# First four feature-column products of a decoder layer made before the norm: r and shift applied at the PSUM read, modulation weights laid out by feature tile

## The chip, the cores and the metric

The kernel runs on one core of a Trainium2 chip. The metric is the device time of one execution in microseconds (us), the median of several. Engines: PE is TensorE (matmul; PEld its weight load), DVE is VectorE, ACT is ScalarE, POOL is GpSimd, SP is SyncE, whose queue issues the DMAs.

## The reference, cut to what matters

A decoder layer for 1024 prompt tokens and 8 decode tokens (T = 1032 columns), D = 1024 features. The part before the token mixers:

```python
mod = (silu(c) @ w_ada + b_ada)                    # 6 x 1024 values: sh1, sc1, gt1, sh2, sc2, gt2
h = rmsnorm(x, g_pre_mix) * (1 + sc1) + sh1        # rmsnorm: x * r(token) * g, r = 1/sqrt(mean(x*x) + eps)
proj = h @ w_in                                    # 1024 -> 2048, in 16 tiles of 128 columns
a_val, a_gate, b_in, c_u, c_v, d_b, d_c, d_h = split(proj, 8)
za = a_val * sigmoid(a_gate)                       # tiles 0, 1 times tiles 2, 3; then a causal conv, 31 taps
...
x = x + gt1 * rmsnorm(out @ w_out, g_post_mix)     # then a SwiGLU FFN with its own norms and modulation
```

The prompt has one c, each decode token its own; so sh1 and sc1 have nine columns per feature.

## The kernel before, in words

Everything is transposed: features lie on the 128 partitions, tokens in the free direction. x is held as KD = 8 feature tiles `xk[k]` of 128 x 1032. The tokens are taken in three column groups c = 0, 1, 2 of W = 344 (the last eight of c = 2 are the decode tokens). Every fp32 product is made of three matmuls: operands are split into a rounded part and a rest (`hh`/`hl`, `wh`/`wl`), and `mm3` (L183 to L188) multiplies hh·wh, hl·wh and hh·wl into one PSUM bank. PSUM has six rotating banks (`psum`) and one double one (`psum_two`). The order of the work on each engine is the order in which the Python code issues it; there is no scheduler, and each engine takes its own queue in order.

The front of the program: all eight x tiles are loaded (`x_load`, L119). ACT squares them and DVE adds the squares into `Sx` (`x_stat`, L369 to L376). `compact_r` (L316) sums over the partitions with matmuls by `ones` (L325), makes r by Newton steps on DVE, spreads it by diagonal matrices `dg` (L336) and matmuls (L338), and ACT copies it to `rx` (L379). The modulation comes in slices of two feature tiles: four pieces of 512 KB each, `ada_mm` (L216 to L220, 32 small matmuls per slice), a copy (`ada_evac`, L224), a turn (`ada_turn`, L229) and `ada_finish` (L232), which leaves sh1 in `mod` and g·(1 + sc1) in `gmul["g1"]`. `modulate_steps` (L402) then makes, for a tile and a column group, tmp = x·G·r on DVE (L405), hh = tmp + sh on ACT (L408) and hl on DVE (L409); for c = 2 POOL does the eight decode columns (L413 to L417).

The first four weight tiles (`IN_ORDER` = 2, 0, 3, 1: gates and values of the conv mixer) are multiplied for c = 0 and most of c = 1 while the modulation still arrives: seven accumulators (five banks and the double one) grow by two feature tiles per slice s (the loop over s, `accs` and `ks`). Then come projection (1, 1) (tile 1, c = 1), five blocks of `v_units` (L628: 128 tokens x 256 columns of w_v, 24 matmuls a block), in whose cover the c = 2 tiles are modulated, the four c = 2 projections, the other four blocks, and the other projections from (6, 0) on. `gate` (L530) and `value` (L535) read the accumulators from PSUM. `ada_rest` makes the remaining modulation slices and `conv_a` (L543) the conv chain on DVE (L550, 58 links) as side generators that `step()` advances between pieces of TensorE work. `compact` (L889) makes the later norms the same way as `compact_r`. `split` (L140) rounds a weight block on ACT (L145) and makes its rest, mostly on POOL (L146).

## Time and profile before

| | |
|---|---|
| median of 3 runs | 1079.89 us (1078.48 to 1080.2) |
| profiled execution, its own time | 1080.22 us |
| span from its first to its last instruction | 1078.5 us |
| busy: PE, DVE, ACT, POOL | 1028.6, 728.7, 373.0, 378.3 us |
| moved by DMA | 169.54 MB, 157 GB/s in the mean |

Times in the rows are us from the start of the span, durations of groups in ns where the view says so. A busy PE is not PE at full speed: the granted clock stands in a row or column of its own. In the timeline a row gives start, duration, engine, line, operation, tiles; in brackets the idle time before it and what ended it. An idle engine costs something only where another waits for its work.

### The profile page before, as it was taken

Reading aid. Unit: us, or ns where it says so; the run is one execution under the profiler, and the core shown is the slowest. Engines: PE = TensorE matmul, PEld = TensorE weight load, DVE = VectorE, ACT = ScalarE, POOL = GpSimd, SP = SyncE. Lnnn points to the kernel's source line nnn. Section 1 sums busy time; section 2 is a strip of 40 time slices with the busy share of each in tenths; the row PEclk is TensorE's granted clock in tenths of the full one; section 3 lists DMA queues with packets and bytes.
Section 4 is the critical chain, followed back from the end, with each engine's and each line's share of the span. In section 5 each row is a group of like instructions: output and inputs, shape, how many; then the busy total and the mean of one; then the engine's idle time right before and its main releaser. Section 6 shows DMA issues by size and latency. Waiting matters only on the chain.

```text
span 1078.5 us, 21308 instructions
## 1 busy us (share of the span) xinstructions
PE 1028.6 (95%) x8658; PEld 1003.7 (93%) x8658; DVE 728.7 (68%) x1318; ACT 373.0 (35%) x732; POOL 378.3 (35%) x338
## 2 busy tenths in 40 slices
PE   4998999999998999999999999999999999999995
PEld 3897888899998899999999999999999999999994
DVE  5483978998336897697666666666667674539476
ACT  4240022114433333333323323323225463436431
POOL 1251144423534433443333323323333344315240
PEclk9999999999998999999999999999999999999997
DMA  9812434572323320256344444344338895646423
GB/s 355 306 41 79 156 112 145 132 176 66 112 79 118 133 92 14 69 183 210 139 167 148 138 168 147 138 168 148 138 128 305 313 322 181 190 157 218 157 89 149
DMA packets 69091, 169.54 MB, mean 157 GB/s; under 512 B 14200, under 2 KB 16128, under 8 KB 68992
## 3 DMA queue, kind: packets, MB, share of 16 engines
q1 hardware_dynamic: 68992, 168.17, 46.1%
q8 instruction: 68, 1.11, 0.4%
q14 instruction: 31, 0.25, 0.1%
HBM read 127.21 MB, written 40.93 MB: 156 GB/s over the span
## 4 chain that ended last, share of the span: by engine, by line
PE 72%; DVE 13%; issue 6%; DMA 3%; ACT 3%; POOL 3%; SPq 0%; POOLq 0%; DVEq 0%; ACTq 0%
PE ps L186 20%; PE ps L187 20%; PE ps L188 20%; PE ps L220 2%; PE pc L187 2%; PE pc L188 2%; PE pc L186 2%; DVE sq L915 1%; DVE pc L550 1%; DMA draw<-a 1%; POOL m L951 1%; PE ps L641 1%; PE ps L642 1%; PE ps L643 1%; DMA adas<-in_wada 1%
## 5 line engine op out<-in xcount | busy, mean ns | idle before, releaser
L186 PE MATMUL ps<-thP,sP 128*128 128x256 f32 (+1 forms) x1064 | 299.7, 282 | 0.7 <-DVE u L1176 0.7
L187 PE MATMUL ps<-tlP,sP 128*128 128x256 f32 (+1 forms) x1064 | 299.6, 282 | 0.0
L188 PE MATMUL ps<-thP,sP 128*128 128x256 f32 (+1 forms) x1064 | 299.4, 281 | 0.0
L186 PEld LDWEIGHTS ps<-thP,sP 128*128 128x128 f32 x1064 | 200.3, 188 | 1.2 <-DVE u L1176 1.1
L188 PEld LDWEIGHTS ps<-thP,sP 128*128 128x128 f32 x1064 | 200.6, 189 | 0.0
L187 PEld LDWEIGHTS ps<-tlP,sP 128*128 128x128 f32 x1064 | 200.3, 188 | 0.0
L186 PE MATMUL ps<-dt,ds 128*128 128x256 f32 (+1 forms) x484 | 136.6, 282 | 0.0
L187 PE MATMUL ps<-dt,ds 128*128 128x256 f32 (+1 forms) x484 | 136.2, 281 | 0.0
L188 PE MATMUL ps<-dt,ds 128*128 128x256 f32 (+1 forms) x484 | 136.1, 281 | 0.0
L1014 POOL TENSOR_TENSOR sP<-ssum,sP 128x512 fp32r<-128x512 f32 x57 | 75.6, 1327 | 147.1 <-ACT sP L1012 145.5
L1265 POOL TENSOR_TENSOR ds<-draw,ds 128x512 fp32r<-128x512 f32 x42 | 71.6, 1707 | 117.1 <-ACT ds L1259 115.0
L186 PE MATMUL ps<-hh,wh 128*128 128x344 f32 x300 | 100.2, 334 | 1.3 <-ACT hh L408 1.2
L187 PE MATMUL ps<-hl,wh 128*128 128x344 f32 x300 | 96.7, 322 | 0.4 <-DVE hl L409 0.4
L188 PE MATMUL ps<-hh,wl 128*128 128x344 f32 x300 | 96.5, 322 | 0.0
L1012 ACT CAST sP<-ssum 128x512 fp32r<-128x512 f32 x76 | 45.4, 620 | 138.4 <-DVE ssum L1047 70.7
L186 PEld LDWEIGHTS ps<-dt,ds 128*128 128x128 f32 x484 | 91.2, 188 | 0.0
L187 PEld LDWEIGHTS ps<-dt,ds 128*128 128x128 f32 x484 | 91.1, 188 | 0.0
L188 PEld LDWEIGHTS ps<-dt,ds 128*128 128x128 f32 x484 | 91.1, 188 | 0.0
L550 DVE SCALAR_TENSOR_TENSOR pc<-za,vec,pc 128x1024 f32<-128x1024 f32 x58 | 74.6, 1286 | 1.4
L1264 DVE TENSOR_TENSOR dt<-draw,dt 128x520 fp32r<-128x520 f32 x77 | 63.9, 854 | 15.7 <-ACT dt L1258 15.6
L1258 ACT CAST dt<-draw 128x520 fp32r<-128x520 f32 x77 | 48.2, 626 | 61.6 <-PE pc L188 40.4
L146 POOL TENSOR_TENSOR wl<-wr,wh 128x1024 fp32r<-128x1024 f32 x14 | 33.6, 2401 | 89.7 <-ACT wh L145 83.0
(319 smaller groups left out, 2432.4 us busy)
## 6 DMA issues: line engine op xcount, KB each, us to landing
wr<-in_wada SPq DMA_DIRECT2D x32, 512.0 KB, 3.9
t<-tsum SPq DMA_DIRECT2D x22, 520.0 KB, 3.1
draw<-t SPq DMA_DIRECT2D x44, 260.0 KB, 5.4
wraw<-in_w_gate SPq DMA_DIRECT2D x22, 512.0 KB, 4.6
wraw<-in_w_up SPq DMA_DIRECT2D x22, 512.0 KB, 5.1
dsum<-in_w_down SPq DMA_DIRECT2D x22, 512.0 KB, 5.6
draw<-s SPq DMA_DIRECT2D x44, 256.0 KB, 5.3
draw<-in_w_down SPq DMA_DIRECT2D x33, 256.0 KB, 5.3
```

Source lines behind the costliest of these rows:

```text
L146: (lo_eng or nc.gpsimd).tensor_tensor(out=lo, in0=raw, in1=hi.bitcast(F32), op=ALU.subtract)
L186: nc.tensor.matmul(out, wh, xh, start=start, stop=False, skip_group_check=more)
L187: nc.tensor.matmul(out, wh, xl, start=False, stop=False, skip_group_check=more)
L188: nc.tensor.matmul(out, wl, xh, start=False, stop=stop, skip_group_check=more)
L220: nc.tensor.matmul(acc[32 * g:32 * g + 32, :P], csil[:, k, :], piece[:, kk, g, :], start=(k == 0), stop=(k == KD - 1))
L550: nc.vector.scalar_tensor_tensor(out=acc if j < 30 else ca[i][:, :SEQ], in0=za[i][:, j:j + SEQ], scalar=v(VCAW + 31 * i + j), in1=acc, op0 ...
L641: nc.tensor.matmul(ps[:m, :GW], hh[k][:, tk], w[0][:, k % 4], start=(k == 0), stop=False)
L1012: nc.scalar.copy(out=t[:, 0], in_=src)
L1014: eng.tensor_tensor(out=t[:, 1], in0=src, in1=t[:, 0].bitcast(F32), op=ALU.subtract)
L1258: nc.scalar.copy(out=t[:, 0], in_=x[:, 1])
L1264: V.tensor_tensor(out=t[:, 1], in0=x[:, 1], in1=t[:, 0].bitcast(F32), op=ALU.subtract)
L1265: (V if k % 2 else nc.gpsimd).tensor_tensor(out=s[:, 1], in0=x[:, 0, :512], in1=s[:, 0].bitcast(F32), op=ALU.subtract)
```

## The change

The products of the first four weight tiles no longer wait for r and for the shift. With G = g·(1 + sc1) and shift sh, W·(x·G·r + sh) = r·(W·(x·G)) + W·sh. So hh/hl first hold the parts of x·G alone (`gained`). Ten extra columns behind c = 1 (`EXTRA`, NX = 10) hold the parts of sh1 itself (nine values and one of padding), and the c = 1 accumulators, 354 columns wide, give W·sh1 in them (`take_bias`). When PSUM is read, DVE multiplies by r (`with_r`) and the bias is added in the sigmoid or in the value's product.

The modulation weights of this part are laid out by feature tile: 16 pieces of 512 KB, a scale and a shift piece for each k, in six rotating buffers. `ada_first` makes the nine (ten) values of a piece with eight small matmuls, an ACT copy and one matmul by `sel`, all in one PSUM bank. x and w_first are loaded tile by tile as well. The sums of squares run beside the products. For all later consumers (v blocks, projections from (6, 0) on) the eight tiles are made a second time, now with r and shift: `scaled` (x·G·r in place: odd k by DVE, even k by POOL and ACT) and `shifted` (hh on ACT, hl on DVE), while projections (1, 0), (2, 2), (0, 2), (3, 2), (1, 2) run. The nine v blocks then stand together, two to a bank. The sums in `compact_r` and `compact` are 8 columns wide instead of 128.

```diff
+        def ada_first(k, what):
+            piece = first_pieces.pop((k, what))
+            acc = psum()
+            for kk in range(2):
+                for g in range(4):
+                    nc.tensor.matmul(acc[32 * g:32 * g + 32, :P], csil[:, 2 * g + kk, :], piece[:, 2 * g + kk, :], start=(kk == 0), stop=(kk == 1))
+            st = sm.tile([P, P], F32, tag="ada", name="ada", bufs=1)
+            nc.scalar.copy(out=st, in_=acc[:, :P])
+            yield
+            tp = acc[:, 256:288]
+            nc.tensor.matmul(tp, st, sel, start=True, stop=True)
...
+            if what:
+                nc.vector.tensor_scalar(out=sh1t[:, k], in0=tp[:, :NX], scalar1=b, scalar2=None, op0=ALU.add)
+            else:
+                t = sm.tile([P, 9], F32, tag="nt", name="nt")
+                nc.vector.tensor_scalar(out=t, in0=tp[:, :9], scalar1=b, scalar2=1.0, op0=ALU.add, op1=ALU.add)
+                nc.vector.tensor_scalar(out=gmul["g1"][:, k], in0=t, scalar1=v(VGPRE + k), scalar2=None, op0=ALU.mult)
...
+        def gained(k, src, dst):
+            nc.scalar.mul(out=hh[k][:, dst], in_=xk[k][:, src], mul=G1[:, k, 0:1])
+            nc.vector.scalar_tensor_tensor(out=hl[k][:, dst], in0=xk[k][:, src], scalar=G1[:, k, 0:1], in1=hh[k][:, dst].bitcast(F32),
+                                           op0=ALU.mult, op1=ALU.subtract)
+        def parts(src, k, dst, eng):
+            nc.scalar.copy(out=hh[k][:, dst], in_=src)
+            eng.tensor_tensor(out=hl[k][:, dst], in0=src, in1=hh[k][:, dst].bitcast(F32), op=ALU.subtract)
+        def scaled(k, cl, r, eng):
+            x = xk[k][:, cl]
+            if eng is nc.vector:
+                eng.scalar_tensor_tensor(out=x, in0=x, scalar=G1[:, k, 0:1], in1=r, op0=ALU.mult, op1=ALU.mult)
+            else:
+                eng.tensor_tensor(out=x, in0=x, in1=r, op=ALU.mult)
+                nc.scalar.activation(out=x, in_=x, func=AF.Identity, scale=G1[:, k, 0:1], bias=sh1(k)[:, 0:1])
+        def shifted(k, cl, eng):
+            x, hi, lo = xk[k][:, cl], hh[k][:, cl], hl[k][:, cl]
+            if eng is nc.vector:
+                nc.scalar.activation(out=hi, in_=x, func=AF.Identity, bias=sh1(k)[:, 0:1])
+                nc.vector.scalar_tensor_tensor(out=lo, in0=x, scalar=sh1(k)[:, 0:1], in1=hi.bitcast(F32), op0=ALU.add, op1=ALU.subtract)
+            else:
+                nc.scalar.copy(out=hi, in_=x)
+                nc.vector.tensor_tensor(out=lo, in0=x, in1=hi.bitcast(F32), op=ALU.subtract)
+        def eng_of(k):
+            return nc.vector if k % 2 else nc.gpsimd
...
-        accs = [(IN_ORDER[j], 0) for j in range(4)] + [(IN_ORDER[j], 1) for j in range(3)]
+        accs = [(n, 0) for n in (2, 3, 0)] + [(n, 1) for n in (2, 3, 0, 1)]
...
-        for s in range(4):
+        for k in range(KD):
             for j, (n, c) in enumerate(accs):
...
+                mm3(first[n, c][:, :gw(c)], w_in[n](k), gx(k, c), k == 0, k == KD - 1)
+                if k < KD - 1:
...
+                    if j == (3 if k == 0 else 1):
+                        g = ada_first(k + 1, 0)
+                        next(g)
+                    if j == (4 if k == 0 else 3):
+                        next(g, None)
+                        gained(k + 1, LO, LO)
+                    if j == 4:
+                        g = ada_first(k + 1, 1)
+                        next(g)
+                        for q in ((k + 1,) if k < 3 else (4, 5) if k == 3 else range(k + 2, min(k + 3, KD))):
+                            x_stat(q)
+                    if j == 6:
+                        next(g, None)
+                        parts(sh1t[:, k + 1], k + 1, EXTRA, nc.gpsimd)
+                if k == 6 and j == 3:
+                    comp = compact_r(Sx, 2 * W, rx_out(rx), big.tile([P, 6, P], F32, tag="y12", name="dg"))
+                    next(comp)
+                    next(comp)
...
+        def with_r(ps, c):
+            t = sm.tile([P, W], F32, tag="tmp", name="tmp", bufs=4)
+            nc.vector.tensor_tensor(out=t, in0=ps[:, :W], in1=rx[:, cols(c)] if c < 2 else rx2, op=ALU.mult)
+            return t
...
+        evac(2, 0)
+        evac(3, 0)
+        next(comp)
+        gained_proj(1, 0)
+        evac(0, 0)
+        gained_proj(2, 2)
+        evac(2, 1)
+        evac(3, 1)
+        for k in range(KD):
+            scaled(k, LO, rx, eng_of(k))
...
+        gained_proj(0, 2, comp)
...
+            shifted(k, LO, eng_of(k))
+        gained_proj(3, 2)
...
+        gained_proj(1, 2)
+        CL2 = slice(2 * W, SEQ)
+        for k in range(KD):
+            scaled(k, CL2, rx2[:, :NP2], eng_of(k))
...
-                nc.tensor.matmul(ps[:, P * b:P * b + P], S[:, t0:t0 + P], ones, start=True, stop=True)
+                nc.tensor.matmul(ps[:, 8 * b:8 * b + 8], S[:, t0:t0 + P], ones[:, :8], start=True, stop=True)
```

**The order on PE, at the start.** Before: the sums over tokens (`ones`, `Sx`), a whole modulation slice, its turn and the diagonals stand ahead of the first product of `hh` and `wh`.

```order
L325 MATMUL ps<-ones,Sx 128x128 x6
L220 MATMUL ps<-adas,csil 32x128 x32
L229 MATMUL ps<-ident,ada 128x128
L338 MATMUL ps<-dg,ones 128x128 x5
L338 MATMUL ps<-dg,ones 128x48
L186 MATMUL ps<-hh_147,wh 128x344
```

In the change one piece (eight matmuls) and its turn stand ahead of it (lines are those of the changed kernel; `w_140` is the first w_first tile):

```order
L224 MATMUL ps<-adas,csil 32x128 x8
L229 MATMUL ps<-sel,ada 128x32
L185 MATMUL ps<-hh_97,w_140 128x344
L186 MATMUL ps<-hl_105,w_140 128x344
L187 MATMUL ps<-hh_97,w_140 128x344
L224 MATMUL ps<-adas,csil 32x128 x8
```

The sums and diagonals have moved behind the products of the seventh and into those of the last feature tile.

**The order on DVE, in the tile loop** of the change (one tile's period; `g_93` is G, `hl_107` the rest of tile 2):

```order
L232 TENSOR_SCALAR sh1t<-ps,vec 128x10
L235 TENSOR_SCALAR nt<-ps,vec 128x9
L236 TENSOR_SCALAR g_93<-nt,vec 128x9
L400 SCALAR_TENSOR_TENSOR hl_107<-x_73,g_93,hh_99 128x688
L386 TENSOR_TENSOR Sx<-Sx,sqx 128x688
```

The sums of squares, which stood ahead of everything, have moved into the loop, behind the rest of each tile and ahead of the next read of a shift.

**The order on POOL, in the second modulation** of the change (`rx_116` is rx2, r for the last 344 columns):

```order
L413 TENSOR_TENSOR x_71<-x_71,rx 128x688
L413 TENSOR_TENSOR x_73<-x_73,rx 128x688
L413 TENSOR_TENSOR x_75<-x_75,rx 128x688
L413 TENSOR_TENSOR x_77<-x_77,rx 128x688
L413 TENSOR_TENSOR x_71<-x_71,rx_116 128x336
```

These are new: before, POOL multiplied only the eight decode columns of a tile. On DVE stand at the same time the odd tiles' `L411` (688 columns, x and rx as inputs) and the eight `L421`/`L424` of the shifted tiles.

## Rows read from the trace of the kernel before

**Rows 1.** The page, part 1: busy us, share of the span and instructions of each engine.

```profile
PE 1028.6 (95%) x8658; PEld 1003.7 (93%) x8658; DVE 728.7 (68%) x1318; ACT 373.0 (35%) x732; POOL 378.3 (35%) x338
```

**Rows 2.** Busy time by stages: stretch, its length, then PE, PEld, DVE, ACT, POOL busy (instructions), granted clock, DMA share, GB/s.

```profile
0.00:10.00 10.00, 0.00 (x0) 0.00 (x0) 3.40 (x6) 5.81 (x8) 0.20 (x4) 1.00 0.81 270
10.00:20.00 10.00, 5.73 (x80) 4.94 (x81) 5.97 (x19) 3.41 (x5) 2.35 (x1) 1.00 1.03 403
20.00:30.00 10.00, 8.29 (x93) 6.98 (x92) 5.47 (x14) 4.23 (x8) 2.37 (x1) 0.83 1.03 409
...
100.00:120.00 20.00, 18.08 (x188) 15.75 (x189) 13.74 (x32) 0.27 (x1) 0.88 (x3) 0.91 0.48 160
...
140.00:160.00 20.00, 20.00 (x188) 17.99 (x187) 13.47 (x15) 4.66 (x9) 12.43 (x11) 1.00 0.31 106
```

**Rows 3.** PE's timeline from 13 to 66: the sums over tokens, the turn of a slice, the first product, products at either level of the clock, the end of projection (1, 1), a v block (every third row of its products).

```profile
13.68 2.93 PE L325 MATMUL ps<-ones,Sx 128*128 128x128 f32 x12 [13.68 <-DVE Sx L376]
...
19.50 0.33 PE L229 MATMUL ps<-ident,ada 128*128 128x128 f32 x1 [0.38 <-ACT ada L224]
...
23.16 0.42 PE L186 MATMUL ps<-hh,wh 128*128 128x344 f32 x1 [1.21 <-ACT hh L408]
...
24.74 0.49 PE L187 MATMUL ps<-hl,wh 128*128 128x344 f32 x1
25.02 0.49 PE L188 MATMUL ps<-hh,wl 128*128 128x344 f32 x1
...
30.54 0.32 PE L188 MATMUL ps<-hh,wl 128*128 128x344 f32 x1
30.70 0.32 PE L186 MATMUL ps<-hh,wh 128*128 128x344 f32 x1
...
64.07 0.83 PE L325 MATMUL ps<-ones,Sx 128*128 128x128 f32 x6
...
65.10 0.28 PE L641 MATMUL ps<-whx,hh 128*128 128x256 f32 x1
...
65.45 0.28 PE L641 MATMUL ps<-whx,hh 128*128 128x256 f32 x1
```

**Rows 4.** The chain of waits, 0 to 125: start, length, what.

```profile
10.60 7.83 DMA adas<-in_wada
...
98.63 3.25 DMA wr<-in_wada
101.92 0.71 PE ps L220 x16
...
117.82 0.57 PE ps L220 x16
118.39 0.35 PE ps L186
```

**Rows 5.** The DMA view, 0 to 60: GB/s in 40 slices of 1.5 us.

```profile
GB/s 0 179 299 301 334 402 409 376 418 410 401 423 401 407 415 401 421 393 410 412 404 412 410 407 419 369 377 338 316 350 359 168 0 76 273 0 0 0 0 5
```

**Rows 6.** Groups of instructions, 0 to 130, by line and shape: count, busy us, mean ns of one, idle before.

```profile
L409 DVE SCALAR_TENSOR_TENSOR hl<-tmp,mod,hh 128x344 fp32r<-128x344 f32 x16 | 8.5, 574 | 1.3 <-ACT hh L408 1.3
L376 DVE TENSOR_TENSOR Sx<-Sx,sqx 128x688 f32<-128x688 f32 x7 | 6.1, 875 | 3.6 <-ACT sqx L375 3.1
L336 DVE TENSOR_SCALAR dg<-ident,nr 128x128 f32<-128x128 f32 x9 | 2.2, 282 | 1.3 <-PE ps L338 1.3
L408 ACT ACTIVATE hh<-tmp,mod 128x344 fp32r<-128x344 f32 x16 | 8.6, 582 | 10.9 <-DVE tmp L405 10.9
L145 ACT CAST whx<-wr 128x1024 fp32r<-128x1024 f32 x2 | 2.0, 1038 | 0.0
L224 ACT COPY ada<-ps 128x128 f32<-128x128 f32 x6 | 1.6, 265 | 41.5 <-PE ps L220 41.5
```

**Rows 7.** POOL's timeline from 70 to 80 (two products of the decode columns), and the DVE row beside the first.

```profile
70.59 0.52 POOL L414 TENSOR_TENSOR td<-td,rx 128x8 f32<-128x8 f32 x1 [4.67 <-ACT rx L379]
...
79.41 0.20 POOL L414 TENSOR_TENSOR td<-td,rx 128x8 f32<-128x8 f32 x1
...
70.49 1.05 DVE L405 SCALAR_TENSOR_TENSOR tmp<-x,g,rx 128x336 f32<-128x336 f32 x2 [1.03 <-ACT rx L379]
```

**Rows 8.** Single lines with the least, median and greatest duration in ns, and three rows of the timeline: POOL's wlx, and a later pair on POOL and DVE.

```profile
L376 DVE TENSOR_TENSOR Sx<-Sx,sqx x14: 517/875/2534, 6.5 to 60.3; 128x688 f32<-128x688 f32 x7, 128x344 f32<-128x344 f32 x7
L1014 POOL TENSOR_TENSOR sP<-ssum,sP x57: 1285/1297/1894, 435.4 to 813.9; 128x512 fp32r<-128x512 f32 x57
...
59.85 5.21 POOL L146 TENSOR_TENSOR wlx<-wr,whx 128x1024 fp32r<-128x1024 f32 x2 [10.36 <-ACT whx L145]
826.62 1.72 POOL L1265 TENSOR_TENSOR ds<-draw,ds 128x512 fp32r<-128x512 f32 x1 [1.20 <-ACT ds L1259]
827.10 1.79 DVE L1264 TENSOR_TENSOR dt<-draw,dt 128x520 fp32r<-128x520 f32 x1
```

**Rows 9.** PE's timeline at a later compact (two column sums of 128 columns, then the next product) and at two 8-column fp32 matmuls.

```profile
294.95 0.60 PE L895 MATMUL ps<-ones,sq 128*128 128x128 f32 x4
295.31 0.36 PE L186 MATMUL ps<-ya,whx 128*128 128x256 f32 x1
...
185.75 0.28 PE L732 MATMUL ps<-td,poolw 128*128 128x8 f32 x2
185.89 0.40 PE L186 MATMUL ps<-hh,wh 128*128 128x344 f32 x1
```

More of the change, by code (lines that the diff above doesn't have):

```diff
@@ L329, in compact_r @@
             small_rsqrt(m9[:, :nb], nb, r9[:, :nb], 1.0 / D, RMS_EPS)
-            yield
+            for b in range(nb):
+                nc.vector.tensor_scalar(out=dg[:, b], in0=ident, scalar1=r9[:, b:b + 1], scalar2=None, op0=ALU.mult)
             for b0 in range(0, nb, 4):
+                yield
                 ps = psum()
@@ L334, in compact_r @@
                 for b in range(b0, min(b0 + 4, nb)):
-                    dg = sm.tile([P, P], F32, tag="dg", name="dg")
-                    nc.vector.tensor_scalar(out=dg, in0=ident, scalar1=r9[:, b:b + 1], scalar2=None, op0=ALU.mult)
                     skip = P * b - offs[b]
-                    nc.tensor.matmul(ps[:, w0:w0 + P - skip], ones, dg[:, skip:], start=True, stop=True)
+                    nc.tensor.matmul(ps[:, w0:w0 + P - skip], ones, dg[:, b, skip:], start=True, stop=True)
                     w0 += P - skip
@@ new lines, in build, with x_square @@
+        G1 = gmul["g1"]
+        Sx = big.tile([P, 2 * W], F32, tag="y13", name="Sx")
+        Sx2 = sm.tile([P, W], F32, tag="tmp", name="Sx2", bufs=4)
+        rx = sm.tile([P, 2 * W], F32, tag="nw", name="rx", bufs=1)
+        rx2 = const.tile([P, W], F32, tag="p3", name="rx2")
+        hd = const.tile([P, KD, ND], F32, name="hd")
+        LO, EXTRA, HI2 = slice(0, 2 * W), slice(2 * W, 2 * W + NX), slice(2 * W, T)
+        NP2 = W - ND
+        def x_square(k, S, cl, sq, eng):
+            if k == 0:
+                nc.scalar.activation(out=S, in_=xk[k][:, cl], func=AF.Square)
+            else:
+                nc.scalar.activation(out=sq, in_=xk[k][:, cl], func=AF.Square)
+                eng.tensor_tensor(out=S, in0=S, in1=sq, op=ALU.add)
@@ L493, in build @@
+                if k == 7 and j == 6:
+                    comp = compact_r(Sx2, W, rx_out(rx2), sm.tile([P, 3, P], F32, tag="tmp", name="dg", bufs=4))
+                    next(comp)
+        gained(KD - 1, slice(2 * W, SEQ), slice(2 * W, SEQ))
+        nc.gpsimd.tensor_tensor(out=hd, in0=hd, in1=G1[:, :, 1:9], op=ALU.mult)
+        for k in range(KD):
+            parts(hd[:, k], k, slice(SEQ, T), nc.gpsimd)
         sgut = load([P, 4, P], a["sgut"], "sgut", "p0")
@@ L628, in v_units @@
         def v_units(wv):
[L629 removed]
+            for grp in ((0, 1, 2, 3), (4, 5, 6, 7), (8,)):
                 ng = len(grp)
@@ L800, in build, with gained_proj, evac @@
         fns = {2: gate(0), 0: value(0), 3: gate(1), 1: value(1)}
-        for n, c in ((2, 0), (3, 0), (2, 1), (3, 1), (0, 0), (1, 0), (0, 1)):
-            proj(n, c, fns[n])
-        proj(1, 1, fns[1])
+        def gained_proj(n, c, g=None):
+            ps = first[n, c] = psum()
+            for k in range(KD):
+                if k == 3 and g is not None:
+                    next(g, None)
+                mm3(ps[:, :W], w_in[n](k), gx(k, c), k == 0, k == KD - 1)
+        def evac(n, c):
+            fns[n](first.pop((n, c)), c)
+        for n in (2, 3, 0, 1):
+            take_bias(n)
+        evac(2, 0)
+        evac(3, 0)
+        next(comp)
+        gained_proj(1, 0)
[3 more added lines that the diff above has]
+        evac(3, 1)
+        for k in range(KD):
+            scaled(k, LO, rx, eng_of(k))
+        evac(0, 1)
+        evac(1, 1)
+        evac(1, 0)
+        gained_proj(0, 2, comp)
+        for k in range(4):
+            shifted(k, LO, eng_of(k))
+        for k in range(4, KD):
+            shifted(k, LO, eng_of(k))
+        gained_proj(3, 2)
+        evac(2, 2)
+        evac(0, 2)
+        evac(3, 2)
+        gained_proj(1, 2)
+        CL2 = slice(2 * W, SEQ)
+        for k in range(KD):
+            scaled(k, CL2, rx2[:, :NP2], eng_of(k))
+        nc.gpsimd.tensor_tensor(out=hd, in0=hd, in1=rx2[:, None, DS].to_broadcast([P, KD, ND]), op=ALU.mult)
+        nc.gpsimd.tensor_tensor(out=hd, in0=hd, in1=sh1t[:, :, 1:9], op=ALU.add)
+        evac(1, 2)
         c_start()
```

320 lines of the change are left out of this document (142 added, 178 removed).

## The prediction, made before the changed kernel had run

> **What bounds the kernel now.** I read the page first: TensorE is busy 95% of the span, the other engines 35 to 68% [rows 1]. What is left to gain lies at the start, so the table by stages comes next: no TensorE work in the first 10 us, 5.73 in the second 10, a clock of 0.83 in the third, and short idle or slow stretches up to 120 [rows 2]. Then TensorE's timeline [rows 3]: the first product of a feature tile starts at 23.16, projection (1,1) ends at 64.07. The chain of waits says why it starts so late: a modulation piece lands at 18.4 [rows 4]; the sums over tokens, which waited for DVE until 13.68, the turn, the diagonals and rx all stand ahead of the first product [rows 3]. In the same chain the first product of projection (6,0), after which the program hardly differs, starts at 118.39. My sum is made up to there, in the profiled execution (1080.22 us by its own time, span 1078.5; the median of the runs is 0.33 lower).
>
> **The head start.** Ahead of the first product the change leaves 1.45 MB of loads (c, vec, ident, the decode columns, one x, one w_first piece, one modulation piece). The bandwidth row gives 0.27, 0.45, 0.45 and 0.50 MB in the slices of 1.5 us up to 7.5 [rows 5], so they are in at 6.9. Then eight small matmuls (0.57, [rows 4]), copy (0.27), turn (0.33) [rows 3, 6], two small DVE operations (estimated 0.4), the ACT write of hh (0.58) [rows 6] and hops: first product at about 9.4. **Gain 13.7 us.**
>
> **The tile loop.** The number of products stays: 21 per tile. At full clock they follow each other in 0.157, at the lower level (1.2 GHz) in 0.286 [rows 3]. TensorE has just been idle, so tile 0 is paid at 0.286, with its second piece in between: 8.3 us. Later tiles cost TensorE 21 × 0.157 + 2 × 0.57 (pieces, [rows 4]) + 0.2 = 4.65. But one PSUM bank (five hold accumulators, two more belong to the double one) serves both pieces of a tile, so the steps form a ring: shift read out by DVE 0.2, piece 0.67, six products 0.95, turn 0.3, gain on DVE 0.45, ACT hh of 688 columns 0.86, DVE hl 0.93, DVE sum of squares 0.88, and the shift's read again. The 0.86 and 0.93 are estimates: 2 × the 0.53 at which 344-column operations follow each other [rows 7] less one fixed part; the 0.88 is a row [rows 6]. Together 5.25, with two sums in tiles 3 and 4 0.9 more. So tile 7's gain is turned at T = 48.9. **About 8 us of the head start go here** (3.7 in tile 0, 0.6 in each later one, and the two sums).
>
> **The tail of the tiles.** In DVE's queue stand hl of tile 7, the Newton steps (12 × an estimated 0.2) and six diagonals (6 × 0.28 at most, [rows 6]) ahead of tile 7's shift; its extra columns come 2.3 late. The second group of diagonal matmuls needs the bank that ACT's first rx copy frees, and seven ACT operations of up to 0.58 [rows 6] stand before it: 1.8. The sums for the last 344 columns wait for the second rx copy, behind two weight casts of 1.04 [rows 6]: 1.4. Projection (1,0) needs a bank that DVE frees only after the rx copies, four bias copies and one product with rx: 1.9. With the work between, it starts at T + 15.85 and ends at T + 19.6 = 68.5, where before stood at 64.07 [rows 3]. **Here 13.7 of gain have become a loss of 4.4.**
>
> **The second modulation.** LO (688 columns) and the last 336 of all eight tiles are made again, with r and shift, before the v blocks. Four projections of 24 × 0.157 = 3.77 cover it: the first v block could end at T + 38.6. The work: POOL multiplies four tiles of 688 and four of 336 columns. No POOL multiply of that size is in the trace; at the 1.29 of its 512-column ones [rows 8] I take 1.72 and 0.85, 10.3 together. DVE has four scaled tiles and eight shifted ones of about 0.93 and the value products: 12 from T + 24, when POOL has done wlx (2 × 2.4) and the decode columns. Can these run at once? A DVE sum (L376, 344 columns) that takes 0.52 alone took 2.53 in the stretch of POOL's wlx; DVE's L1264 took 1.79 beside a POOL L1265 that took 1.72, where POOL needs 1.3 for 512 columns [rows 8]. A POOL product of eight columns took 0.52 while DVE's L405 ran, and 0.20 when DVE had done with them [rows 7]. So the two exclude each other in the one form (tensor_tensor) in both directions, and POOL waits for the other (scalar_tensor_tensor); whether that other form waits for a long POOL operation no row shows. If all of it goes one by one, hl of tile 7 is there at T + 24 + 10.3 + 12 = T + 46.5, and the first v block ends at T + 47, 8 late; if only the tensor_tensor half waits, at T + 40.5, 2 late. I take the first, since the rows nearest to it (L405, L409 against L414) are of that form. The Trainium skill ("SBUF — State Buffer", section "Who interferes with whom") says that a DVE instruction with two SBUF inputs contends with a GpSimd instruction that reads SBUF, and that whoever issues first holds the pair of ports for the whole instruction. By that rule all of it goes one by one; it speaks against giving half of the tiles to POOL.
>
> From there eight more v blocks of 24 × 0.118 = 2.85 [rows 3], some seven pieces of 0.57 [rows 4] and a stretch at the lower clock, as after the stall of 98.63 to 101.92 [rows 4], where 16 small matmuls still took 0.71: 2 us. T + 47 + 22.8 + 4 + 2 = 124.7. **Projection (6,0) starts at about 125 instead of 118.39: +6.5.**
>
> **What costs nothing or little.** The compacts' sums become 8 columns wide: a 128-column one takes 0.18 (two in 0.36), an 8-column one 0.14 [rows 9], and the later compacts have 30 by the code; 30 × 0.04 = **−1.2**, from 0 to at most 30 × 0.18 = −5.4. The ten extra columns: 96 × 0.157 × 10/344 = 0.4, counted in the 4.65. The conv chain on DVE (each link 1.286) starts some 6 us later; DVE is idle for 6.5 us in 140 to 160 [rows 2], which covers it; without them they would come on top. The pieces' loads: 16 × 512 KB with x and w_first at the 400 GB/s of [rows 5] are in by 39, and the last is needed at 45. SP's queue gets no longer; a fetch of the later slices behind POOL's weight split could repeat the 3.25 stall of [rows 4], which is as long as the one it replaces.
>
> Sum: 1080.22 + 6.5 − 1.2 = 1085.5; less 0.33, **1085 us**. The bounds: if only half of the second modulation waits, 6 less (1079); if the lower clock holds through the gaps of the tile loop, some 8 more (1093).
>
> **Rivals.** *(B) POOL and DVE run side by side.* Then hl of tile 7 comes at about T + 39, 7.5 earlier, there is no stall and no clock loss after it: projection (6,0) starts at 116 and the time is 1076.5, faster. For it: scalar_tensor_tensor is never seen waiting for POOL. Against: [rows 7, 8]. It decides as soon as scaled and shifted operations of DVE keep 0.93 beside POOL's. *(C) The tiles run at TensorE's pace.* If the ring is no longer than 4.65 (the estimated 0.86 and 0.93 would have to be 0.6) and the tail is half as long, T is 44 and projection (1,0) ends at 58: most of the head start is kept and the second modulation has 10 us more, 1069. For it: in 10 of the 20 us behind the first product nothing but the pieces held TensorE up (8.29 busy in 20 to 30, with the late start in it, [rows 2]). Against: before, a whole slice of two tiles was made ahead of need, now one bank and one tile. *(D) The clock falls in the tile loop.* In 20 to 30 it was granted at 0.83 after an idle start [rows 2]; if gaps of 0.6 in every 5.3 us keep products at 0.286, each such tile costs 2.7 more; three or four of them make 1094. Against: 100 to 120 had gaps as well and 0.91.
>
> **How the numbers follow.** The forecast (all serialized) 0.52, B 0.25, C 0.13, D 0.10. A measurement of this kernel can tell about 0.2% (2 us) from no change. Forecast: 0.85 slower, 0.08 same, 0.07 faster; B 0.80 faster, 0.10 same; C nearly all faster; D all slower. That makes faster 0.36, same 0.08, slower 0.56. The range goes from C (1070) to D (1094), since B, C and the unknown half of the second modulation lie inside and about 0.1 is left at either end; the forecast's own is 1079 to 1091.
>
> **What would show it.** Right: first product near 9.4; tile periods of 5.2 to 5.5 with TensorE waiting on hh and hl; a gap before projection (1,0) behind rx; DVE's and POOL's 688-column operations at two or more times their lone duration around 70 to 95; the first v block stalled on hl; projection (6,0) near 125. Wrong: tile periods under 4.8, or (1,0) ending before 62; 688-column DVE operations at 0.93 beside POOL's 1.7; projection (6,0) before 117; a granted clock of half speed through several tiles; or any difference after projection (6,0) beyond the 1.2 of the compacts.

## The result, and the profile after

The changed kernel takes 1093.66 us (median; 1093.48 to 1097.13), the kernel before 1079.57 beside it: 1.0135 times as long, 95% interval 1.0116 to 1.0153. The forecast was 1085.0, slower by 5.4 us. The direction is right, the size is not: the profiled execution takes 1093.53, against 1080.22 that is **+13.3**. Two single executions far above the rest (4491.42 us in run 1, 1134.57 of the kernel before beside run 15) are left out of the ratios.

The page after, part 1 (the same columns as [rows 1]), and the table by stages (as [rows 2]):

```profile
PE 1040.3 (95%) x8686; PEld 1009.6 (92%) x8686; DVE 749.8 (69%) x1329; ACT 391.9 (36%) x791; POOL 391.3 (36%) x344
```

```profile
0.00:10.00 10.00, 1.08 (x16) 0.66 (x16) 0.90 (x3) 2.52 (x4) 1.47 (x5) 1.00 0.76 225
10.00:20.00 10.00, 7.81 (x69) 5.60 (x69) 2.21 (x7) 3.34 (x9) 1.48 (x2) 1.00 1.03 408
20.00:30.00 10.00, 10.00 (x101) 8.55 (x98) 4.25 (x9) 5.05 (x12) 3.00 (x4) 1.00 1.04 402
...
140.00:160.00 20.00, 20.00 (x187) 18.21 (x182) 19.09 (x29) 3.15 (x7) 7.19 (x8) 1.00 0.24 76
160.00:180.00 20.00, 16.95 (x146) 15.14 (x145) 10.54 (x12) 4.52 (x10) 8.42 (x9) 0.91 0.41 138
```

In the first 30 us TensorE does work for 18.9 us where before it did 14.0: the head start is real. But it is now busy in all of 20 to 30, so there is no idle time left there in which added work could hide, and in 140 to 160 DVE is busy for 19.09 of 20 (before 13.47) while a gap opens in 160 to 180.

PE's timeline after, from the first modulation piece to the late gap (start, length, what; in brackets the idle time before and who ended it):

```profile
8.66 1.08 PE L224 MATMUL ps<-adas,csil 128*32 128x128 f32 x16 [8.66 <-DMA adas<-in_wada]
...
11.95 0.66 PE L185 MATMUL ps<-hh,w 128*128 128x344 f32 x1 [1.20 <-ACT hh L399]
...
14.89 0.49 PE L186 MATMUL ps<-hl,w 128*128 128x344 f32 x1
15.18 0.47 PE L187 MATMUL ps<-hh,w 128*128 128x344 f32 x1
...
15.65 0.32 PE L186 MATMUL ps<-hl,w 128*128 128x344 f32 x1
15.81 0.32 PE L187 MATMUL ps<-hh,w 128*128 128x344 f32 x1
...
26.81 0.41 PE L185 MATMUL ps<-hh,w 128*128 128x344 f32 x1
...
27.70 0.32 PE L187 MATMUL ps<-hh,w 128*128 128x344 f32 x1
27.95 0.65 PE L224 MATMUL ps<-adas,csil 128*32 128x128 f32 x16
...
28.79 0.32 PE L186 MATMUL ps<-hl,w 128*128 128x344 f32 x1
...
29.43 0.32 PE L187 MATMUL ps<-hh,w 128*128 128x354 f32 x1
29.59 0.30 PE L229 MATMUL ps<-sel,ada 128*128 128x32 f32 x2
...
29.97 0.33 PE L186 MATMUL ps<-hl,w 128*128 128x354 f32 x1
...
32.17 0.40 PE L185 MATMUL ps<-hh,w 128*128 128x344 f32 x1
...
39.66 0.64 PE L224 MATMUL ps<-adas,csil 128*32 128x128 f32 x16 [0.85 <-DVE sh1t L232]
...
52.89 0.30 PE L229 MATMUL ps<-sel,ada 128*128 128x32 f32 x2
...
66.97 1.42 PE L327 MATMUL ps<-ones,Sx 128*128 128x8 f32 x6 [0.99 <-ACT rx L395]
68.65 0.65 PE L185 MATMUL ps<-hh,w 128*128 128x344 f32 x1 [0.25 <-DVE ns L328]
...
72.54 0.49 PE L186 MATMUL ps<-hl,w 128*128 128x344 f32 x1
72.83 0.49 PE L187 MATMUL ps<-hh,w 128*128 128x344 f32 x1
...
126.73 0.43 PE L185 MATMUL ps<-hh,wh 128*128 128x344 f32 x1
...
164.36 0.65 PE L247 MATMUL ps<-wr,csil 128*32 128x128 f32 x16 [3.05 <-DMA wr<-in_wada]
...
212.06 0.64 PE L247 MATMUL ps<-wr,csil 128*32 128x128 f32 x16
```

Six things are to be seen in it.

1. The first product starts at 11.95, not at 23.16.
2. Products follow each other in 0.29 until 15.5 (the lower level of the clock) and in 0.16 behind it, although the clock column of the stage says 1.00: the spacing of the products shows the level, that column did not.
3. Tile 2 starts at 26.81 and tile 3 at 32.17, a period of 5.36 in which no row has a bracket, so **TensorE does not wait there**.
4. What an interruption costs: one piece between products takes 27.70 to 28.79 less two products, 1.09 − 0.31 = 0.77, and a turn 29.43 to 29.97 less two products, 0.23.
5. In the tile with two sums of squares on DVE, TensorE waits 0.85 for the read of the shift (39.66); one such sum takes 0.87.
6. The turn of tile 7's gain, which is the prediction's T, is at 52.89. Projection (1,0) starts at 68.65 behind waits for ACT's rx and DVE, and it runs at the lower level again (72.54 to 72.83).

Against the markers of before (first product 23.16; 60.28, where its next projection follows on the seven accumulators; 64.07, where that projection ends; 118.32, the first product of (6,0)), the difference after less before goes:

| marker | after | before | difference | added in the step |
|---|---|---|---|---|
| first product | 11.95 | 23.16 | −11.2 | −11.2 |
| seven accumulators done | 65.8 | 60.28 | +5.5 | +16.7 |
| next projection starts | 68.65 | 60.28 | +8.4 | +2.9 |
| it ends | 74.7 | 64.07 | +10.6 | +2.3 |
| projection (6,0) starts | 126.73 | 118.32 | +8.4 | −2.2 |
| end (by the spans) | 1091.8 | 1078.5 | +13.3 | +4.9 |

The pieces' price could be read before the change: in the old kernel's timeline of PE, one piece between products takes 39.25 to 40.33 less two products, 0.77 as well:

```profile
39.25 0.31 PE L188 MATMUL ps<-hh,wl 128*128 128x344 f32 x1
39.49 0.65 PE L220 MATMUL ps<-adas,csil 128*32 128x128 f32 x16
...
40.33 0.32 PE L187 MATMUL ps<-hl,wh 128*128 128x344 f32 x1
...
118.32 0.42 PE L186 MATMUL ps<-hh,wh 128*128 128x344 f32 x1
...
198.96 0.65 PE L220 MATMUL ps<-wr,csil 128*32 128x128 f32 x16
```

The last two rows, and 126.73 and 212.06 of the change, bound the same work from projection (6,0) to a later modulation piece: 80.64 before, 85.33 after. The 4.7 between them lie in the stretch of the late gap.

DVE after, in the second Newton solve, in the second modulation and in the convolution (start, length, what), and POOL beside it:

```profile
73.46 1.51 DVE L302 TENSOR_TENSOR nt<-np,nt 128x3 f32<-128x3 f32 x1
75.01 1.59 DVE L303 SCALAR_TENSOR_TENSOR ny<-nt,ny 128x3 f32<-128x3 f32 x1
76.63 1.58 DVE L307 TENSOR_TENSOR nt<-ny 128x3 f32<-128x3 f32 x1
...
89.65 1.58 DVE L424 TENSOR_TENSOR hl<-x,hh 128x688 fp32r<-128x688 f32 x1
...
94.48 0.86 DVE L424 TENSOR_TENSOR hl<-x,hh 128x688 fp32r<-128x688 f32 x1
...
145.05 7.92 DVE L607 SCALAR_TENSOR_TENSOR pc<-za,vec,pc 128x1024 f32<-128x1024 f32 x6
152.87 0.68 DVE L735 TENSOR_TENSOR sgt<-ps,sgub 128x512 f32<-128x512 f32 x1
```

```profile
73.29 6.53 POOL L413 TENSOR_TENSOR x<-x,rx 128x688 f32<-128x688 f32 x4
...
153.69 1.30 POOL L737 TENSOR_TENSOR cu<-cu,sgt 128x512 f32<-128x512 f32 x1 [7.60 <-issue]
```

Four DVE operations on three columns last 1.5 to 1.6 each while POOL multiplies 688 columns in 6.53/4 = 1.63. The first two remainder operations of 688 columns take 1.58 beside POOL's multiplies of 336; 0.86 is what one takes behind them.

The chain of waits after, at the late gap (start, length, what):

```profile
154.94 2.42 POOL wl L145
...
157.80 6.52 DMA wr<-in_wada
```

Six convolution links stand in DVE's queue ahead of the sum L735 (145.05 to 152.97). POOL's product L737 needs that sum and waits 7.60 for it. POOL's weight split L145 stands behind the product and ends at 157.36. Only then is the next slice fetched (157.80 to 164.32), and TensorE waits 3.05.

### The profile page after: what moved, and what is told of

Read it like the earlier page. It is cut to its first block, busy times and chain, and to the rows that moved or that the text cites. A ratio compares the mean times of both kernels' runs of the same rounds, so it can differ in the third digit from the quotient of the medians.

```text
span 1091.8 us, 21476 instructions
## 1 busy us (share of the span) xinstructions
PE 1040.3 (95%) x8686; PEld 1009.6 (92%) x8686; DVE 749.8 (69%) x1329; ACT 391.9 (36%) x791; POOL 391.3 (36%) x344
## 4 chain that ended last, share of the span: by engine, by line
PE 65%; DVE 15%; issue 6%; ACT 2%; POOL 2%; DMA 1%; SPq 0%; POOLq 0%; ACTq 0%; DVEq 0%
PE ps L185 20%; PE ps L186 20%; PE ps L187 20%; DVE pc L607 2%; PE pc L186 1%; PE pc L185 1%; PE pc L187 1%; DVE sq L1012 1%; DVE h L1064 1%; DVE h L1023 1%; DMA wr<-in_wada 1%; PE ps L992 1%; POOL m L1048 1%; DVE vn L715 1%; POOL wl L145 0%
## 5 line engine op out<-in xcount | busy, mean ns | idle before, releaser
L1109 ACT CAST sP<-ssum 128x512 fp32r<-128x512 f32 x76 | 45.4, 620 | 137.7 <-DVE ssum L1144 70.2
L185 PE MATMUL ps<-hh,wh 128*128 128x344 f32 x240 | 79.9, 333 | 0.0
L1361 DVE TENSOR_TENSOR dt<-draw,dt 128x520 fp32r<-128x520 f32 x77 | 67.1, 896 | 14.5 <-ACT dt L1355 14.4
L187 PE MATMUL ps<-hh,wl 128*128 128x344 f32 x240 | 76.9, 321 | 0.0
L186 PE MATMUL ps<-hl,wh 128*128 128x344 f32 x240 | 76.9, 320 | 0.0
L1279 POOL TENSOR_TENSOR act<-u,u 128x256 f32<-128x256 f32 (+1 forms) x38 | 28.8, 758 | 59.2 <-ACT u L1278 59.2
```

What stands on the lines that cost most here:

```text
L185: nc.tensor.matmul(out, wh, xh, start=start, stop=False, skip_group_check=more)
L186: nc.tensor.matmul(out, wh, xl, start=False, stop=False, skip_group_check=more)
L187: nc.tensor.matmul(out, wl, xh, start=False, stop=stop, skip_group_check=more)
L1109: nc.scalar.copy(out=t[:, 0], in_=src)
L1279: nc.gpsimd.tensor_tensor(out=at[m][:, 1, g, :w], in0=e["u2"], in1=e["u3"], op=ALU.mult)
L1361: V.tensor_tensor(out=t[:, 1], in0=x[:, 1], in1=t[:, 0].bitcast(F32), op=ALU.subtract)
```

## The experiments

Each was run beside the kernel before on the same chip; ratios are to that. Three are edits of the kernel before, the others of the changed kernel or of one another.

**1. All scaled and shifted tiles of the second modulation on DVE and ACT, none on POOL.**

```
     def eng_of(k):
-        return nc.vector if k % 2 else nc.gpsimd
+        return nc.vector
```

> The changed kernel with all scaled and shifted tiles made by DVE and ACT alone: POOL's eight multiplies by r (4 x 1.63 and 4 x 1.2 us) are gone, DVE has 5.5 us of scaled tiles more. Theory (DVE operations with two SBUF inputs wait for a whole POOL multiply): the twelve small Newton operations for the second r fall from up to 1.59 to 0.2 us each, the diagonals for it come 5 to 6 us earlier, the first v block ends 2 to 3 earlier, 1090 to 1092 us in all. Rival (these operations are slow for another reason, or POOL's work was truly in parallel): the Newton operations stay long, or DVE's 5.5 us come on top, 1096 to 1099.

1094.77 us, 1.0137 [1.0116, 1.0158]. DVE's timeline in the second Newton solve of this kernel:

```profile
75.78 0.16 DVE L302 TENSOR_TENSOR nt<-np,nt 128x3 f32<-128x3 f32 x1
75.98 0.16 DVE L303 SCALAR_TENSOR_TENSOR ny<-nt,ny 128x3 f32<-128x3 f32 x1
```

The exclusion is shown: 1.51 and 1.59 become 0.16 with POOL's multiplies away. Projection (6,0) started at 125.03, 1.7 earlier, although the clock rose only at 25 in this execution (15.5 after). The time didn't follow: the late gap was still there with 3.3, and waits of 0.94 (for vn) and 0.75 (for wl) came beside it, so that by 204 this kernel was 0.9 behind the change.

**2. The tail in another order**: rx copies and the second sums ahead of the last gained columns and of the weight casts, two projections' banks emptied before them.

```
-                if k == 7 and j == 4:
-                    w_split()
...
-        for n in (2, 3, 0, 1):
+        for n in (2, 3):
             take_bias(n)
+            evac(n, 0)
+        comp = compact_r(Sx2, W, rx_out(rx2), ...)
+        next(comp)
...
+        for q in range(2, KD):
+            gained(q, slice(2 * W, SEQ), slice(2 * W, SEQ))
+        w_split()
```

> The changed kernel with another order in the queues behind the last feature tile: on ACT the copies of rx come ahead of the last six gained writes and of the two weight casts; on DVE the read of tile 7's shift comes ahead of the six diagonals and the products with rx of (2,0) and (3,0) ahead of the sums for the second r. Theory (queue order makes the gap before projection (1,0), and the gap makes the low clock behind it): projection (1,0) starts at 62 to 63 instead of 68.65 and runs at full clock; 1085 to 1088 if TensorE's order is then the bound. Rival 1 (DVE's second modulation is the bound behind it): the gap goes, but the first v block comes only 3 to 5 earlier: 1089 to 1091. Rival 2 (POOL's wlx and multiplies now meet the Newton steps): 1092 to 1095.

1094.8, 1.0139 [1.0121, 1.0157]. The projection behind the tiles started 3.5 earlier relative to T, and a new wait of 5.3 stood in projection (2,2): the decode columns' hh and hl were now queued on POOL behind the split wlx, by my order.

**3. The product cu × sgt (L737) on DVE instead of POOL.**

```
-                nc.gpsimd.tensor_tensor(out=cu[i][:, tk], in0=cu[i][:, tk], in1=..., op=ALU.mult)
+                nc.vector.tensor_tensor(out=cu[i][:, tk], in0=cu[i][:, tk], in1=..., op=ALU.mult)
```

> The changed kernel with the spatial gate's product cu = cu * sgt on DVE instead of POOL, nothing else. Theory (the late stall of TensorE at 161 comes from POOL's queue: this product waits there for DVE, which is behind with its conv links, and the weight split behind it frees the buffer that the next modulation load needs): the stall of 3.05 us and the low clock behind it go, 1088 to 1090. Rival (the load waits for SP's queue or for bandwidth): the stall stays, 1093 to 1095, or DVE's 2.8 us more come on top.

1090.57, 1.0101 [1.0079, 1.0122]: 0.34% or 3.6 us under the change's ratio, though the ends of the two intervals overlap. The timeline is clearer. POOL's weight split of this kernel starts 8.4 earlier and TensorE has no wait in 160 to 180:

```profile
146.53 2.40 POOL L145 TENSOR_TENSOR wl<-wr,wh 128x1024 fp32r<-128x1024 f32 x1 [0.77 <-ACT wh L144]
```

From projection (6,0) to the piece that stands at 212.06 in the change, PE needs 80.65 in this kernel, as before (80.64) and not as in the change (85.33):

```profile
127.29 0.43 PE L185 MATMUL ps<-hh,wh 128*128 128x344 f32 x1
...
207.94 0.65 PE L247 MATMUL ps<-wr,csil 128*32 128x128 f32 x16
```

One edit, of one instruction's engine, takes the late gap away.

**4. All three (1, 2 and 3).**

> The three edits before together. If they are three separate losses: 1093.7 - 2.5 - 6 - 4.5 = 1080 to 1082. If the pieces of modulation inside the tile loop (15 interruptions) have used up the head start and the waits behind only replace one another: 1086 or more.

1089.68, 1.0093 [1.0074, 1.0112]. From (6,0) on it runs nearly like the kernel before: from the second product of (6,0), at 127.20, to 207.05 it needs 79.85, before 79.5. With run 3 this makes the late gap the cause of the table's last step. The head of the program kept its loss: the wait of 5.3 was still there.

**5. As 4, the decode columns ahead of the w_v splits.**

```
-        w_split()
-        w_split()
-        w_fetch()
         nc.gpsimd.tensor_tensor(out=hd, in0=hd, in1=G1[:, :, 1:9], op=ALU.mult)
...
+        w_split()
+        w_split()
+        w_fetch()
```

> The three edits together (as in the run before them), with one order put right: POOL and ACT make the gained decode columns before the two weight splits of w_v and not behind them, where projection (2,2) waited 5.3 us for them in both runs that had the tail's new order. Theory (queue order): that wait and the low clock behind it (76.3 to 83.2) go, so 1089.7 - 5.3 - 2 to 3 = 1081 to 1083, no wait over 1 us is left on TensorE before 200, and projection (6,0) starts near 119 to 121. If 1081 is reached and no more, the head start of 11 us has been paid back by TensorE's own added work (the 15 interruptions by pieces and what stood ahead of the first product before). Rival (DVE's second modulation binds next): a new wait of 3 us or more on hl or x in the projections or the first v blocks, 1085 to 1088.

1090.32, 1.0089 [1.0066, 1.0111]: no gain over run 4 that could be told. The wait of 5.3 is gone and one of 2.3 has come, on a bank that DVE frees behind Newton operations that met wlx:

```profile
72.86 2.41 DVE L302 TENSOR_TENSOR nt<-np,nt 128x3 f32<-128x3 f32 x1
```

**6. As 5, both pieces of a tile back to back**, one copy and one read of PSUM for both.

```
-                        g = ada_first(k + 1, 0)
+                        g = ada_pair(k + 1)
```

> The run beside it, with the scale and the shift piece of a tile multiplied one behind the other (16 small matmuls, one copy, two turns in a row) instead of apart: 7 interruptions of the products fewer. Theory (an interruption costs TensorE more than its matmuls: 0.77 for eight small matmuls whose own time is 0.57, and 0.23 for a turn): the tile's period falls from 5.36 by 0.3 to 0.5, 2 to 3.5 us in all below the run beside it. Rival (the ring of waits over one bank sets the period): as long or longer, since the pair holds the bank longer: 5.4 to 6 a tile, 0 to +5 us.

1093.02, 1.0118 [1.0104, 1.0132]: by the ratios 3.1 us worse than 5, with intervals that just overlap. TensorE now waited 0.55 for hl in each of six tiles of the loop, 3.3 in all: the tile's input is made in one go, late.

**7. The sums of squares behind the read of the shift**, out of the ring that I had summed to 5.25.

```
                     if j == 4:
...
-                        for q in (...):
-                            x_stat(q)
                     if j == 6:
                         next(g, None)
                         parts(sh1t[:, k + 1], k + 1, EXTRA, nc.gpsimd)
+                        for q in (...):
+                            x_stat(q)
```

> The changed kernel with DVE's sum of squares behind the read of the shift instead of ahead of it, in each tile. The prediction's ring of waits (5.25 us, 0.88 of it this sum): the period falls to TensorE's own 4.65, 5 us less in all, 1088. Rival (TensorE itself needs 5.36 a tile: 21 products of 0.159, two pieces of 0.77, two turns of 0.23): no change of the period, only the wait of 0.9 in the tile with two sums goes: 1092.5 to 1094.

1094.33, 1.0133 [1.0119, 1.0147]. The turns of the shift on PE in this kernel still come every 5.37 us:

```profile
27.35 0.30 PE L229 MATMUL ps<-sel,ada 128*128 128x32 f32 x2
...
32.72 0.30 PE L229 MATMUL ps<-sel,ada 128*128 128x32 f32 x2
```

TensorE's own work is enough to set the period. It does not follow that the ring is shorter than the prediction had it: the 0.85 at 39.66 in the change is nearly all of a second sum's 0.87, so the ring had almost no slack either. The two are about equal, and shortening one of them alone gains nothing.

**8. The kernel before, with the compacts' sums 8 columns wide and nothing else.**

```
-                nc.tensor.matmul(ps[:, P * b:P * b + P], S[:, t0:t0 + P], ones, ...)
+                nc.tensor.matmul(ps[:, 8 * b:8 * b + 8], S[:, t0:t0 + P], ones[:, :8], ...)
```

> The kernel before with this part of the change alone: the sums over partitions in the later norms (compact) 8 columns wide instead of 128. Prediction's term: 30 x 0.04 = 1.2 us less, 1078.5 against 1079.7. Rival (these matmuls stand where TensorE waits for the Newton steps anyway, or a matmul's start costs as much as its 128 columns): no difference, within 0.3 us.

1080.65 against 1080.13, 1.0004 [0.9996, 1.0013]: the term of −1.2 is zero. PE's timeline of this kernel at a later compact (compare [rows 9]): two sums of 8 columns take 295.79 to 296.15, the same 0.36 as two of 128.

```profile
295.79 0.51 PE L895 MATMUL ps<-ones,sq 128*128 128x8 f32 x4
296.15 0.37 PE L186 MATMUL ps<-ya,whx 128*128 128x256 f32 x1
```

**9. The change with 16 idle products (ones × ones) on TensorE ahead of everything.**

```
+        def warm(n):
+            ps = psum()
+            for _ in range(n):
+                nc.tensor.matmul(ps[:, :P], ones, ones, start=True, stop=True)
+        warm(16)
```

> The changed kernel with 16 matmuls of ones by ones ahead of the first modulation piece, where TensorE is idle until 8.7 us; nothing reads them. In the profiles so far the granted clock first rose at 15.5 in the changed kernel and between 18.5 and 25 in its variants, so that up to 10 us of the head start's products ran at half rate. Theory (what TensorE does before sets when the clock rises): full clock at the first product, 3 to 5 us less in the loop, 1089 to 1091, and less spread from run to run. Rival (the time of the rise has nothing to do with these): no change, 1093 to 1095, or later by the matmuls that are not done by 8.7.

1092.03, 1.0104 [1.0087, 1.0121]: between the theory and its rival, and not clear of the change's interval. In PE's timeline of this kernel the first piece finds TensorE 2.21 us idle behind the idle products; the stage 10 to 20 was granted 0.61:

```profile
9.17 0.65 PE L231 MATMUL ps<-adas,csil 128*32 128x128 f32 x16 [2.21 <-DMA adas<-in_wada]
```

**10 and 13. Kernel 5 with the w_v splits in tile 7 and two more banks emptied early; 10 with the 16 idle products, 13 without.**

```
+                if k == 7 and j == 2:
+                    w_split()
+                    w_split()
+                    w_fetch()
...
         next(comp)
+        evac(2, 1)
+        evac(3, 1)
```

> The kernel of the three edits with the decode columns ahead (1090.3), and three edits more: the 16 matmuls of ones; (2,1) and (3,1) are read from PSUM ahead of the gained last columns and the Newton steps of the second r (there the diagonals waited 2.3 us for a bank and the clock fell behind it); the weight splits of w_v come earlier, so that POOL's two long operations do not meet those Newton steps (two of them took 2.4 and 2.3 us). Theory: 2.3 and 1.7 and 3 us less, 1083 to 1085. Rival (DVE, busy 95 to 98% from 70 to 130, is the bound there): only the clock's part is won, 1087 to 1089.

> The kernel of e10 without the matmuls of ones: the three edits, the decode columns ahead, the earlier PSUM reads of (2,1) and (3,1) and the earlier weight splits. Against 1090.3 without the last two and 1085.1 with the matmuls of ones too. If the last order edits carry the 5 us: 1085 to 1086. If the matmuls of ones carry them: 1089 to 1090.

10: 1085.12, 1.0056 [1.0036, 1.0076]; 13: 1087.47, 1.0072 [1.0046, 1.0098]. By the ratios the tail's order gives 1.8 us over kernel 5 and the idle products 1.7 more, but the intervals overlap, and the executions of one kernel differ by more than that: the nine of run 10 go from 1082.81 (mean granted clock 0.984) to 1091.38 (0.976), the six of run 13 from 1083.14 to 1090.69.

**11. The kernel before with 32 idle products.**

> The kernel before with 32 matmuls of ones by ones at the start, where TensorE is idle until 13.7 us. There the sums from 13.68 to 17.0 ran at the lower clock, and 23.9 to 27.3 again. Theory (earlier work brings the full clock earlier): the sums and diagonals ahead of the first product take 1.5 us less, and the low stretch behind may go: 1077 to 1078.5 against 1080.1. Rival (the low stretch only moves, or the chain there goes through DVE and ACT and not through TensorE): within 0.5 us of before.

1078.33 against 1078.83, 0.9992 [0.9982, 1.0002]: no difference.

**12. Kernel 5 without the pieces of tiles 1 to 7** (it leaves out their modulation: G and shift of these tiles come from tile 0's columns).

```
+            if k == 0:
                 piece = first_pieces.pop((k, what))
...
+            else:
+                first_pieces.pop((k, what))
+                tp = sh1t[:, 0]
```

> The kernel of the three edits with the decode columns ahead (1090.3), in which the modulation of tiles 1 to 7 is left out (G and shift come from tile 0's by DVE; the pieces are loaded but not multiplied, turned or copied). Theory (TensorE's own added work, 14 pieces and turns of 1.0 us in the loop, has paid back the head start): the period of a tile falls from 5.36 to the 4.15 at which 1.66 MB per tile come in at 400 GB/s, or to TensorE's 3.4; 8 to 13 us less: 1077 to 1082. Rival (the second modulation on DVE sets the time whatever the loop does): 1086 to 1090.

1079.56, 0.9997 [0.9986, 1.0009], some 10 us under kernel 5. A tile of this kernel lasts 4.46 on PE, waiting 0.15 for hl:

```profile
35.60 0.43 PE L186 MATMUL ps<-hl,w 128*128 128x344 f32 x1 [0.15 <-DVE hl L406]
...
40.06 0.43 PE L186 MATMUL ps<-hl,w 128*128 128x344 f32 x1 [0.15 <-DVE hl L406]
```

So ACT and DVE can keep a period of 4.46. This says nothing against the ring of 5.25, since the run takes two of the ring's parts away as well (the piece, 0.67, and the turn, 0.3). Even without this work the program is only level with before: what 14 pieces and turns cost, 10 us, is about the whole head start.

**14. Kernel 13 with 24 idle products and five more behind the first turn.**

> The kernel of e10 with 24 instead of 16 matmuls of ones at the start and 5 more behind the first turn, so that TensorE has next to no idle time before its first product (with 16 it was idle for 2.2, 0.4 and 1.2 us, and the granted clock, full from 5.3, fell again at 10 to 12 and stayed low until 26). Theory (what TensorE did just before sets the clock): full clock through tiles 0 and 1, 1081 to 1083, and a spread of under 3 us. Rival (the low stretch comes whatever stands there): 1085 to 1087 with the spread of e10 (1082.8 to 1091.4).

1083.25, 1.0034 [1.0023, 1.0046], the fastest variant of the change that does all of its work, 4.2 us under 13. PE's timeline of this kernel in tile 0:

```profile
13.65 0.32 PE L193 MATMUL ps<-hl,w 128*128 128x344 f32 x1
13.81 0.32 PE L194 MATMUL ps<-hh,w 128*128 128x344 f32 x1
```

Its products follow each other in 0.16 here already, and so to 53.9.

**15. The kernel before with 46 and 6 of them:**

> The kernel before with 46 matmuls of ones at the start and 6 behind the diagonals, so that TensorE is busy nearly to its first product (with 32 it was idle for 3 us before the sums, the clock, full from 6.2, was low again from 13.0 to 19.8, and 16 small matmuls and the sums ran at half rate: 1078.3). Theory: full clock through the sums, the first slice and the first products: 1 to 2 us less than before's 1079.2 and 0.5 to 1 less than with 32: 1077 to 1078. Rival (the chain goes through a load that lands at 18.4 and through DVE's diagonals, not through TensorE): 1078 to 1079.5.

1082.04 against 1080.48, 1.0021 [1.0007, 1.0034]: no gain there but a small loss, which no run explains; the slowest of its executions have the lowest granted clock (1086.62 at 0.978, 1077.90 at 0.986). No version beat the kernel before by more than the noise.

## Why the prediction was right in sign and short by 8 us

In the profiled execution +5.3 was forecast (6.5 less 1.2) and +13.3 measured. Of the 8.0 that are missing, 1.9 arose ahead of projection (6,0) (+8.4 instead of +6.5), 1.2 are the term of the compacts, and 4.9 arose behind (6,0), where the prediction had booked nothing else. A difference there beyond 1.2 was one of the prediction's own signs of being wrong. Ahead of (6,0) larger errors cancelled: projection (1,0) ended at 74.7 and not at 68.5, 6.2 late, and from there to (6,0) it took 52.0 where 56.2 had been forecast. That (6,0) came within about 2 us is luck.

*The head start* was forecast at 9.4 and came at 11.95. The step that failed is the loads: the piece's matmuls started at 8.66, not 6.9, which is 1.8 of the 2.5. [rows 5] was read as a rate that holds for any mix, while now the small loads go first. In the trace after, 119 GB/s moved from 3 to 4 us, before 303. By 8.66 the queues had moved some 1.75 MB, more than the 1.45 that had to be there, so loads issued behind the piece shared the bandwidth with it. That the order of the loads is the reason is argued from this and not tested. The rest is the clock: the piece took 1.08 and the turn 0.63 at the lower level, where 0.57 and 0.33 were priced.

*The tile loop* has the right period by luck. I priced TensorE at 4.65 and let a ring of 5.25 bind. The ring was sized about right, but TensorE's own work is as long: the timeline shows no waits in a tile with one sum, and run 7 takes a part out of the ring and nothing moves. The price that failed is 2 × 0.57 for the pieces, their own time in a row: what they take from the stream is 0.77 each, and a turn 0.23 where I allowed 0.1. 21 × 0.159 + 2 × 0.77 + 2 × 0.23 = 5.3. Before, 12 pieces stood in this stretch, mostly three or four in a row, where three cost 1.66; now it is 15, one by one, with two turns to a tile. That run 12 gives 10 us back when 14 pieces and turns go shows their weight. Of the +16.7 in the table some 7.7 are pieces and turns (15 × 1.0 now, about 7.3 before), 2.6 the sums and diagonals that now stand between products, and 3.5 longer waits; this split is an estimate from the two timelines. Tile 0 took 9.3 against 8.3, and T came at 52.89 instead of 48.9.

*The tail of the tiles* has the right sum: (1,0) at T + 15.76 against T + 15.85, behind rx, as said. This is partly luck too. The four delays of the prediction add up to 7.4, while the brackets of TensorE between T and 68.65 add up to 3.0; products at the lower level, from 56.6 to 59.8, fill part of the difference. (1,0) ended at T + 21.8 against T + 19.6: the clock at the lower level behind the gap was priced nowhere.

*The second modulation* was priced too high: from the end of (1,0) to the end of the first v block it took 23.6 and not 27.4 (the block ended at T + 45.4 against T + 47). Run 1 shows that POOL and DVE exclude each other, in both forms of DVE operation: the scalar_tensor_tensor of L303 waits too, on which [rows 7, 8] were silent. The rule that the prediction took from the Trainium skill ("SBUF — State Buffer", "Who interferes with whom") holds here, by 1.59 us for an operation that takes 0.16 alone. But I had the large operations wait. Those lost about 1.6 in all, as four of them, the scaled tiles of DVE, met no POOL multiply; four small ones of the Newton solve lost 5.6. Run 1 shows that undoing it gains no time, as DVE must then do the work. Rival B falls with this. Of rival C half came true, the tiles run at TensorE's pace, but that pace is 5.3 and not 4.65. Of D, products at half clock, there was some in tile 0 and at 57 to 60 and 68 to 73, less than it would need.

*What costs nothing or little* is the step that failed most. The compacts' −1.2 is 0 (run 8): the 0.14 of [rows 9], of another matmul with 8 columns, did not carry over. And "DVE is idle for 6.5 us in 140 to 160 [rows 2], which covers it" took idle time for cover without asking what stands behind the links: with the convolution later, six links stand ahead of L735 and POOL's split waits behind it. I had named the late fetch and said that it would replace the stall of [rows 4]. That stall, at 98.63, did go, but the forecast of (6,0) had already left it out, and this one came on top: 3.05 us and products at 0.29 behind it, 4.7 of the 4.9. Run 3 takes it away and gives 3.6 back by the ratios; behind (6,0) its timeline is that of before.

What stays open: full clock starts at different times in kernels with the same beginning (15.5 after, 17.9 in run 3, 25.2 in run 1; each is one execution), which moves the end of the tile loop: the column sums that start at 53.52 in the change stand 41.6 behind its first product, in run 1 44.8. Only in run 14 was it there from the first products on. What decides it is not shown, and as the executions of one kernel spread as widely (1087.60 to 1093.14 in run 5), the small differences between runs 4, 5, 10 and 13 can't be split further.

## What to carry to other kernels

Price a step that cuts a stream of products by the distance between the products on either side of it, in a timeline, and not by its own row. Before idle time on an engine is booked as cover, follow the queue: what stands behind the work that will move there, on that engine and on those that wait for it, up to the next fetch. A head start is worth what the stream can keep of it: here 11 us were given back in 15 pieces, in sums and waits between the products and in a tail, and the start itself ran at the lower level of the clock. Where two limits are of equal length, as the ring and TensorE's own work here, shortening one of them gains nothing (run 7).

## What the runs showed of the hardware that was not expected

A small operation pays for a large neighbour: 128x3 on DVE takes 0.16 alone (run 1), 1.59 beside POOL's multiply (the change) and 2.41 beside POOL's wlx (run 5). Column sums by TensorE in f32, each with weights of its own, cost 0.18 with 8 columns (run 8) as with 128 ([rows 9]). With idle products ahead of the first work TensorE's products were 0.16 apart by 13.65 (run 14), and yet in run 9, where TensorE was idle for 2.21 us behind them, products were at the lower level from 12.4 to 25.8. Before the first rise the clock column can read 1.00 while products are 0.29 apart (the change, 10 to 15.5).
